# RWKV-7 and neighbourhood attention trunk: mixed inputs stored from GpSimd, two additions moved there, and the second stream's input blocks placed in reverse

## The chip, the cores and the metric

The kernel runs on one core of a Trainium2 chip. The metric is the device time of one execution in microseconds, the median of several runs. TensorE (PE) multiplies matrices; VectorE (DVE), ScalarE (ACT) and GpSimd (POOL) work element by element; SyncE (SP) issues transfers, and so does GpSimd. Each engine runs its own rows strictly in order, and waits on semaphores for what the others and the transfers have to finish first.

## The reference

Two streams (`x_prompt`, `x_sample`, each 512 tokens of width 1024) pass two layers. The change lies in the first steps of layer 0:

```python
def _rms_norm(x, g):
    y = x32 * lax.rsqrt(jnp.mean(x32 * x32, axis=-1, keepdims=True) + RMS_EPS) * g
...
def _rwkv7_branch(xn, mu, w_r, w_k, w_v, w_z, ...):
    x_prev = jnp.pad(xn[:, :-1], ((0, 0), (1, 0), (0, 0)))
    x_next = jnp.pad(xn[:, 1:], ((0, 0), (0, 1), (0, 0)))
    xx = 0.5 * (x_prev + x_next) - xn
    lerp = lambda j: xn + xx * mu[j]
    r = heads(lerp(0) @ w_r)
    k = heads(lerp(1) @ w_k)
    v = heads(lerp(2) @ w_v)
    z = xn @ w_z
    ...
    for d in range(2):      # forward and backward
        ...                 # decay and learning rate from two low-rank products
        ys.append(_wkv7_scan(r, decay, k_d, v, -kk, kk * a, reverse=(d == 1)))
    ...
    return (y * silu(z)) @ w_o
```

Layer 1 is a neighbourhood attention on a grid of 8 x 64 tokens with a gate, and each layer sits between two RMS norms. All is in float32.

## The kernel before, in words

Everything lies transposed: a block is 128 channels by 512 tokens (256 KB), and a stream's x has eight blocks. A product in float32 is made of three matmuls, of a high and a low half of either factor (`whi`, `wlo` for the weights, split by ACT and DVE from the loaded `raw`; L457 to L459 in the prelude, L937 to L939 later). A column is one block of an output: 8 x 3 matmuls, then a copy by ACT and a store to a DRAM tile (`dz`, `dk`, `dr`, `dv`).

The **prelude** comes first. `prelude(0)` normalises stream 0. `prelude(1)` does the same for stream 1, by these steps: it loads x into eight tiles `xn`; ACT squares each block and L472 adds the squares into `acc`; L485 sums over channels on PE; L490 to L499 take the root, the reciprocal and spread it on PE; L568 scales the blocks; L575 adds each token's two neighbours into `xx`. Then `mixed` makes 32 mixed inputs: eight for v of stream 0, and three (k, r, v) for each block of stream 1. Of each, ACT makes the first half (L701), DVE the second (L704), into a place of the ring `ls`, which has four places, and L353 stores it to a DRAM tile (`dlk`, `dlr`, `dlv`, with the stream and block as digits); the normalised x itself is stored for z (`dlz`). All of these are loaded again later as inputs of products. Meanwhile PE makes the columns of z, then k, then r for stream 0. The tiles `xn`, `xx`, `ls` and a few more lie in a memory pool of their own.

The order of rows on each engine in the prelude is set by a scheduler, which follows its own timeline of costs and dependences. When the prelude's code is through, its pool is closed, and the **scan phase** takes the same memory for its own tiles: `k`, `rb`, `r`, `sz`, `MT` and more. A load into such a tile has to wait until the prelude's tile that lay there has been read for the last time. The scan phase's order is woven by hand and by a planner; its first steps are the loads of `rb` and `k` for the first pair of heads, and L1012, which multiplies them on DVE.

A store goes to SP's queue in the prelude (other than the r columns', which come when the scan phase has begun in program order and `away` is set: these go to GpSimd's).

Of the kernel before, what the change touches and what calls it, by code (L numbers as in the profile page):

```python
# [12 lines left out]
F32 = mybir.dt.float32  # L13
F32R = mybir.dt.float32r
AF = mybir.ActivationFunctionType
ALU = mybir.AluOpType
# [4 lines left out]
P = 128  # L21
T = 512
D = 1024
KT = D // P
# [230 lines left out]
class Trunk:  # L255
# [97 lines left out]
        self.store(kind).dma_start(d, src)  # L353

    def store(self, kind):
        return self.nc.gpsimd if kind == "hid" or self.away and kind not in ("y", "x1", "h") else self.nc.sync

    def load(self, dst, src):
        self.nc.sync.dma_start(dst, src)
# [172 lines left out]
    def prelude(self, s):  # L532
        nc = self.nc
        vt, gps, act = nc.vector, nc.gpsimd, nc.scalar
        xs = []
        if s == 0:
            self.vectors()
        for k in range(KT):
            if s == 0 and k == self.WFIRST:
                self.first = [self.weight(self.a["w_z"][0])]  # L540
            t = self.t("xn", (P, T + 2), 16, F32, self.lp)
            self.load(t[:, 1:T + 1], self.a["x"][s][k * P:(k + 1) * P, :])
            xs.append(t)
            if s == 0:

                lo, hi = self.pair()
                act.activation(hi, t[:, 1:T + 1], AF.Identity, scale=self.vec("pre0", k))
                vt.scalar_tensor_tensor(lo, t[:, 1:T + 1], self.vec("pre0", k), hi.bitcast(F32), op0=ALU.mult, op1=ALU.subtract)
                self.xz.append((hi, lo))
                yield  # L550
        if s == 0:
            self.consts()
        acc = self.t("acc") if s else self.t("vs", bufs=self.NVS)
        for k, t in enumerate(xs):
            gps.memset(t[:, 0:1], 0.0)
            gps.memset(t[:, T + 1:T + 2], 0.0)
            self.sumsq(acc, t[:, 1:T + 1], k, vt if s or k % 2 else vt)
            yield
        for _ in range(s * self.HOLD):
            yield  # L560
        rstd = self.rstd(acc, (lambda: self.mm) if s else None)
        if s == 0:
            self.rstd0 = rstd
        yield
        xn, xx = [], []
        for k, t in enumerate(xs):
            x = t[:, 1:T + 1]
            vt.scalar_tensor_tensor(x, x, self.vec("pre0", k), rstd, op0=ALU.mult, op1=ALU.mult)  # L568
            xn.append(x)
            yield  # L570
        if s == 0:
            yield from self.lora_weights()
        for k, t in enumerate(xs):
            u = self.t("xx", (P, T), 16, F32, self.lp)
            vt.tensor_tensor(u, t[:, 2:T + 2], t[:, 0:T], op=ALU.add)  # L575
            xx.append(u)
            yield
        self.shift[s] = xn, xx

        if s:  # L580
            for k in range(KT):
                self.mixed(0, "v", 2, k, self.mm)
                yield
            for k in range(KT):
                for kind, j in (("k", 1), ("r", 0), ("v", 2)):
                    self.mixed(s, kind, j, k)
                    yield
                self.save("lz", s, k, xn[k])
            return
        pm = self.p("pf", (P, 2, T))  # L590
        ps = (self.p("pm"), self.p("us"))
        for k in range(KT):
            hi, lo = self.xz[k]
            for q2 in range(2):
                for out, w in ((pm[:, q2], self.wm), (ps[q2], self.wl)):
                    a, b = (m[:, k % 4] for m in w[2 * q2 + k // 4])
                    nc.tensor.matmul(out, a, hi, start=(k == 0), stop=False)
                    nc.tensor.matmul(out, a, lo, start=False, stop=False)
                    nc.tensor.matmul(out, b, hi, start=False, stop=(k == KT - 1))
                yield  # L600
        for k in range(KT):
            hi, lo = (self.t("lw", (P, 4, 2, 64), 16, F32R, self.lp).rearrange("p k q c -> p (k q c)") for _ in range(2))
            t = self.t("xr", bufs=self.NXR)
            self.lerp(t, xn[k], xx[k], 8 + k)
            self.xk.append(self.halves(t, lo, hi))
            yield
        for q2 in range(2):
            mw = self.t("lm", (P, T + 2), 1, F32, self.lp)
            lr = self.t("lr", (P, KT * P), 1, F32, self.lp)
            y, u = lr[:, 0:T], lr[0:64, T:2 * T]  # L610
            gps.memset(mw[:, 0:1], 0.0)
            gps.memset(mw[:, T + 1:T + 2], 0.0)
            vt.tensor_tensor(mw[:, 1:T + 1], pm[:, q2], rstd, op=ALU.mult)
            vt.tensor_tensor(y, mw[:, 2:T + 2], mw[:, 0:T], op=ALU.add)
            yield
            vt.scalar_tensor_tensor(mw[:, 1:T + 1], y, 0.5, mw[:, 1:T + 1], op0=ALU.mult, op1=ALU.subtract)
            vt.tensor_tensor(y, ps[q2], rstd, op=ALU.mult)
            vt.tensor_tensor(y, y, mw[:, 1:T + 1], op=ALU.add)
            for q in (2 * q2, 2 * q2 + 1):
                act.activation(u, y[64 * (q % 2):64 * (q % 2) + 64], AF.Tanh if q < 2 else AF.Copy)  # L620
                self.hidden(q, u)
            yield

    def mixed(self, s, kind, j, k, past=None):

        xn, xx = self.shift[s]
        t = self.t("ls", (P, T), 4, F32, self.lp)
        self.lerp(t, xn[k], xx[k], 8 * j + k, past)
        self.save("l" + kind, s, k, t)

# [1453 lines left out]
```

## Time and profile before

| | |
|---|---|
| median of three runs | 1604.6 us (1599.76 to 1607.57) |
| profiled execution | 1611.46 us, span 1609.7 us |
| PE busy | 1514.1 us, 94% of the span |
| VectorE busy | 1221.7 us, 76% |
| ScalarE busy | 968.9 us, 60% |
| GpSimd busy | 199.9 us, 12% |
| moved by DMA | 343.61 MB, 213 GB/s |

PE is busy nearly all the time. The page's share of an engine is a mean over the whole span; the prelude, to which the change belongs, ends at about 168 us, so views of that stretch alone say more than the page. In a timeline row stand start, length, engine, line and operation, and in brackets how long the engine stood idle before it and what released it. A tile's name is followed by the name of what is read; `d` ahead of a name marks its DRAM tile.

### The profile page before, as it was taken

How to read it: one execution, taken by the hardware profiler on the slowest of the kernel's cores; microseconds unless marked ns; L12 is line 12 of the kernel's file. 1: busy time of each engine (PE TensorE's matmuls, PEld its weight loads, DVE VectorE, ACT ScalarE, POOL GpSimd, SP SyncE). 2: the span in 40 equal slices, each digit the busy share in tenths (PEclk: the TensorE clock that was granted, in tenths of full speed). 3: DMA queues.
4: the chain of work that ended last, by engine and by line, in shares of the span. 5: the costliest groups of instructions: out<-in, count | busy, mean ns of one | idle time of the engine just before them, and what ended most of it. 6: DMA issues, size and time to landing. Idle time of an engine off the chain costs nothing.

```text
span 1609.7 us, 46432 instructions
## 1 busy us (share of the span) xinstructions
PE 1514.1 (94%) x18756; PEld 1171.0 (73%) x18756; DVE 1221.7 (76%) x2714; ACT 968.9 (60%) x1931; POOL 199.9 (12%) x368
## 2 busy tenths in 40 slices
PE   7988789998898999988999999999999999999998
PEld 6866667666676776766777777777777788777776
DVE  8986579678889798877899899665767585664664
ACT  6667455855747566665577665444667665464562
POOL 0000114301111012131001011000110002111110
PEclk9999899999999999999999999999999999999999
DMA  7359677766676788669678675565865347665553
GB/s 244 105 176 319 199 257 246 236 217 214 220 250 221 224 266 262 207 210 299 215 245 284 222 231 190 165 212 167 284 221 178 116 152 231 217 194 189 170 171 111
DMA packets 183670, 343.61 MB, mean 213 GB/s; under 512 B 25888, under 2 KB 58912, under 8 KB 183456
## 3 DMA queue, kind: packets, MB, share of 16 engines
q1 hardware_dynamic: 158272, 256.75, 49.9%
q0 software_dynamic: 25184, 83.90, 14.6%
q8 instruction: 147, 2.41, 0.6%
q14 instruction: 67, 0.55, 0.1%
HBM read 230.33 MB, written 107.09 MB: 210 GB/s over the span
## 4 chain that ended last, share of the span: by engine, by line
PE 58%; DVE 7%; DMA 5%; ACT 4%; issue 3%; SPq 0%; DVEq 0%; ACTq 0%
PE pg L459 7%; PE pg L457 6%; PE pg L458 6%; PE pm L937 6%; PE pm L938 4%; PE pm L939 4%; PE pf L1249 2%; PE sc L1588 2%; PE po L1621 2%; PE pt L1606 2%; PE us L1368 2%; PE zy L1321 2%; PE zy L1372 1%; PE us L1348 1%; DMA cab<-dab 1%
## 5 line engine op out<-in xcount | busy, mean ns | idle before, releaser
L937 PE MATMUL pm<-act,whi 128*128 128x512 f32 x672 | 296.7, 442 | 9.4 <-issue 4.8
L939 PE MATMUL pm<-act,wlo 128*128 128x512 f32 x672 | 268.3, 399 | 13.6 <-DVE wlo L858 13.6
L938 PE MATMUL pm<-act,whi 128*128 128x512 f32 x672 | 268.5, 400 | 4.4 <-DVE act L884 4.3
L937 PEld LDWEIGHTS pm<-act,whi 128*128 128x128 f32 x672 | 128.7, 192 | 49.5 <-issue 14.1
L939 PEld LDWEIGHTS pm<-act,wlo 128*128 128x128 f32 x672 | 129.0, 192 | 44.8 <-DVE wlo L858 15.8
L457 PE MATMUL pg<-act,whi 128*128 128x512 f32 x384 | 156.5, 408 | 0.0
L407 DVE TENSOR_TENSOR wlo<-raw,whi 128x512 fp32r<-128x512 f32 x150 | 102.7, 688 | 68.9 <-ACT whi L406 63.5
L459 PE MATMUL pg<-act,wlo 128*128 128x512 f32 x384 | 153.0, 398 | 0.0
L406 ACT CAST whi<-raw 128x512 fp32r<-128x512 f32 x150 | 92.4, 617 | 99.6 <-PE pg L458 64.4
L458 PE MATMUL pg<-act,whi 128*128 128x512 f32 x384 | 152.3, 397 | 0.0
L938 PEld LDWEIGHTS pm<-act,whi 128*128 128x128 f32 x672 | 129.6, 193 | 29.9 <-DVE act L884 6.8
L858 DVE TENSOR_TENSOR wlo<-raw,whi 128x512 fp32r<-128x512 f32 x166 | 113.4, 684 | 33.6 <-ACT whi L856 31.8
L856 ACT CAST whi<-raw 128x512 fp32r<-128x512 f32 x166 | 102.2, 619 | 36.6 <-PE pm L938 29.4
L459 PEld LDWEIGHTS pg<-act,wlo 128*128 128x128 f32 x384 | 72.2, 188 | 18.2 <-issue 4.3
L1148 DVE TENSOR_TENSOR N<-etmp,N 128x30 f32<-128x30 f32 (+14 forms) x240 | 78.8, 328 | 4.6
L1146 DVE TENSOR_TENSOR etmp<-N 128x30 f32<-128x30 f32 (+14 forms) x240 | 78.6, 328 | 4.4
L458 PEld LDWEIGHTS pg<-act,whi 128*128 128x128 f32 x384 | 72.4, 189 | 13.0 <-issue 1.0
L457 PEld LDWEIGHTS pg<-act,whi 128*128 128x128 f32 x384 | 72.2, 188 | 12.5 <-issue 0.7
L1602 ACT ACTIVATE sb<-sb,mx 128x256 f32<-128x256 f32 x128 | 64.1, 502 | 20.7 <-DVE mx L1601 20.1
L1249 PE MATMUL pf<-cab 64*64 64x128 f32 (+1 forms) x2048 | 69.4, 270 | 1.5 <-issue 1.5
L1360 ACT COPY X<-us 64x256 f32<-64x256 f32 x128 | 46.8, 366 | 27.6 <-PE zy L1227 23.7
L1031 ACT ACTIVATE th<-pm,dv 128x512 f32<-128x512 f32 x64 | 43.9, 686 | 30.3 <-PE pm L1028 29.8
(404 smaller groups left out, 3502.8 us busy)
## 6 DMA issues: line engine op xcount, KB each, us to landing
dab<-ab POOLq DMA_DIRECT2D x32, 1024.0 KB, 7.2
cab<-dab SPq DMA_DIRECT2D x64, 512.0 KB
raw<-in_w_in_dram SPq DMA_DIRECT2D x128, 256.0 KB
bias<-in_rpb_dram SPq DMA_DIRECT2D x32, 384.0 KB
raw<-in_w_z_dram SPq DMA_DIRECT2D x32, 256.0 KB
raw<-in_w_k_dram SPq DMA_DIRECT2D x32, 256.0 KB
raw<-in_w_r_dram SPq DMA_DIRECT2D x32, 256.0 KB
k<-dk SPq DMA_DIRECT2D x32, 256.0 KB
```

What stands on the lines that cost most here:

```text
L406: self.nc.scalar.copy(hi, src)
L407: (eng or self.nc.vector).tensor_tensor(lo, src, hi.bitcast(F32), op=ALU.subtract)
L457: nc.tensor.matmul(ps, hi, x[k][0], start=(k == 0), stop=False)
L458: nc.tensor.matmul(ps, hi, x[k][1], start=False, stop=False)
L459: self.mm = nc.tensor.matmul(ps, lo, x[k][0], start=False, stop=(k == KT - 1))
L856: nc.scalar.copy(hi, raw[h])
L858: nc.vector.tensor_tensor(lo, raw.pop(h), hi.bitcast(F32), op=ALU.subtract)
L937: nc.tensor.matmul(ps, hi[:, at], xh, start=(k == 0), stop=False)
L938: nc.tensor.matmul(ps, hi[:, at], xl, start=False, stop=False)
L939: nc.tensor.matmul(ps, lo[:, at], xh, start=False, stop=(k == KT - 1))
L1148: vt.tensor_tensor(N[:, q + 1:, :q], tv, N[:, q + 1:, :q], op=ALU.add)
L1249: end = nc.tensor.matmul(st.f[half(a), h, 0, d, g] if st.last else st.f[half(a), h, :, d, g], ab[half(h), d, g, 2 * e[d] + 1 - a], rt if s ...
```

## The change

Four things change, all in the prelude:

- Stores of the kinds `lk`, `lr`, `lv` and `lz` (40 transfers of 256 KB) go to GpSimd's queue instead of SP's.
- For stream 1, the squares' additions (seven) and the neighbours' (eight) run on GpSimd instead of VectorE.
- Stream 1's blocks get the eight `xn` places in opposite order: block 0 lies where block 7 lay.
- The ring `ls` has five places instead of four.

```diff
     def store(self, kind):
-        return self.nc.gpsimd if kind == "hid" or self.away and kind not in ("y", "x1", "h") else self.nc.sync
+        return self.nc.gpsimd if kind in ("hid", "lk", "lr", "lv", "lz") or self.away and kind not in ("y", "x1", "h") else self.nc.sync
...
+        spots = [self.t("xn", (P, T + 2), 16, F32, self.lp) for _ in range(KT)][::-1] if s else None
         for k in range(KT):
             if s == 0 and k == self.WFIRST:
                 self.first = [self.weight(self.a["w_z"][0])]
-            t = self.t("xn", (P, T + 2), 16, F32, self.lp)
+            t = spots[k] if s else self.t("xn", (P, T + 2), 16, F32, self.lp)
...
-            self.sumsq(acc, t[:, 1:T + 1], k, vt if s or k % 2 else vt)
+            self.sumsq(acc, t[:, 1:T + 1], k, gps if s else vt)
...
-            vt.tensor_tensor(u, t[:, 2:T + 2], t[:, 0:T], op=ALU.add)
+            (gps if s else vt).tensor_tensor(u, t[:, 2:T + 2], t[:, 0:T], op=ALU.add)
...
     def mixed(self, s, kind, j, k, past=None):
-        t = self.t("ls", (P, T), 4, F32, self.lp)
+        t = self.t("ls", (P, T), 5, F32, self.lp)
```

The line numbers of the changed kernel are one higher from L538 on. The names below carry running numbers; the digits in the name of a DRAM tile are stream and block.

On SP, at the end of the prelude, the stores of mixed inputs stand between the loads in the kernel before:

```order
L353 DMA dlv15_382_1473<-ls_381_1470 128x512
L353 DMA dlk16_387_1491<-ls_386_1488 128x512
L353 DMA dlr16_389_1499<-ls_388_1496 128x512
L353 DMA dlv16_391_1507<-ls_390_1504 128x512
L353 DMA dlk17_394_1517<-ls_393_1514 128x512
L353 DMA dlr17_399_1531<-ls_398_1528 128x512
L353 DMA dlv17_408_1552<-ls_407_1549 128x512
L359 DMA rb_453_1714<-drn0_446_1706 64x512 x2
L359 DMA k_451_1712<-dk00_217_949 128x512
L359 DMA r_452_1713<-dr00_442_1683 128x512
```

At the same place in the changed kernel, SP has the loads alone:

```order
L359 DMA raw_463_1764<-in_w_r_dram 128x512
L359 DMA drn0_446_1706<-tmp_438_1672 128x64
L359 DMA raw_470_1790<-in_w_r_dram 128x512
L359 DMA rb_453_1714<-drn0_446_1706 64x512 x2
L359 DMA k_451_1712<-dk00_217_949 128x512
L359 DMA r_452_1713<-dr00_442_1683 128x512
```

The stores are no longer ahead of `rb` and `k`. On GpSimd, whose only transfers there were the stores of r columns (`dr`), they now stand before and behind these:

```order
L353 DMA dlk12_336_1335<-ls_335_1332 128x512
L353 DMA dr00_442_1683<-tmp_441_1681 128x512
L353 DMA dlr12_347_1360<-ls_346_1357 128x512
L353 DMA dlv12_349_1368<-ls_348_1365 128x512
L353 DMA dlk13_352_1378<-ls_351_1375 128x512
L353 DMA dlr13_356_1394<-ls_355_1391 128x512
L353 DMA dr01_462_1744<-tmp_461_1742 128x512
L353 DMA dlv13_358_1402<-ls_357_1399 128x512
L353 DMA dlk14_361_1412<-ls_360_1409 128x512
L353 DMA dlr14_363_1420<-ls_362_1417 128x512
```

Ten more stores follow behind the last row shown, then the memsets of `MT` and the store of r column 2. Ahead of all, GpSimd has the additions: the squares' (L472, in a row with a library row ahead of the first), then eight pairs of a neighbours' addition and the store of that block for z:

```order
L472 TENSOR_TENSOR acc_185_798<-tmp_202_875,acc_185_798 128x512
L576 TENSOR_TENSOR xx_252_1072<-xn_184_789 128x512
L353 DMA dlz10_324_1298<-xn_184_789 128x512
L576 TENSOR_TENSOR xx_253_1077<-xn_183_788 128x512
L353 DMA dlz11_334_1330<-xn_183_788 128x512
```

The first store of a mixed input comes after the eighth pair. On PE, L485 (the sum of squares over channels) stood right ahead of the spreading L499, among the sums of a k column (L759):

```order
L459 MATMUL zy_251_1064<-lw_156_706,wlo_250_1061 128x512
L485 MATMUL pm_229_976<-ones_145,acc_185_798 128x1 x4
L499 MATMUL pm_232_989<-tmp_231_984,ones_145 128x128
L759 MATMUL pm_233_1006<-tmp_218_951,cc_143 32x128 x4
L499 MATMUL pm_232_989<-tmp_231_984,ones_145 128x128 x3
```

It now stands inside the column before (`zy_228`, with `zy_251` still to come), 38 rows earlier, while L499 keeps its place:

```order
L459 MATMUL zy_228_972<-lw_141_656,wlo_225_965 128x512
L457 MATMUL zy_228_972<-lw_144_666,whi_224_964 128x512
L485 MATMUL pm_229_976<-ones_145,acc_185_798 128x1 x4
L458 MATMUL zy_228_972<-lw_145_667,whi_224_964 128x512
L459 MATMUL zy_228_972<-lw_144_666,wlo_225_965 128x512
```

So some 38 matmuls now stand between the sum and its use. From the border to the scan phase on, the rows of PE, VectorE and ScalarE are the same in both kernels.

## The prediction

> **What bounds the kernel now.** I read the view of windows first, since the change touches only the first 170 of 1609.7 us: behind them TensorE, VectorE and ScalarE have the same rows in the same order in both kernels, and whatever is won or lost before is carried through as it is. Each row gives a stretch, its length, and busy time and instructions of PE, PEld, DVE, ACT and POOL, then granted clock, DMA share and GB/s.
>
> ```profile
> 40.00:80.00 40.00, 40.00 (x177) 32.94 (x176) 38.86 (x64) 26.22 (x46) 0.13 (x2) 1.00 0.33 106
> 80.00:120.00 40.00, 35.63 (x179) 27.17 (x177) 36.25 (x62) 27.79 (x50) 0.00 (x0) 0.91 0.51 174
> 120.00:160.00 40.00, 36.18 (x176) 26.90 (x168) 25.06 (x39) 28.68 (x51) 3.03 (x3) 1.00 0.92 319
> 160.00:200.00 40.00, 30.30 (x237) 23.37 (x238) 21.15 (x30) 18.64 (x38) 7.12 (x12) 0.83 0.59 193
> ```
>
> From 40 to 80 PE never stands. Then it loses 4.4 us, 3.8 us and 9.7 us of each 40, while the DMA engines go from half busy to 0.92. VectorE is nearly full up to 117 us and has room afterwards; GpSimd has almost nothing to do. So the last two rows are where a transfer can be the limit. The view of waits on PE, 150 to 200 us (total, times, longest):
>
> ```profile
> PE pm L939 <- DVE wlo L858: 13.0, 2, 11.5
> ```
>
> One stall of 11.5 us at the border between prelude and scan, the largest here. The releaser named is a weight's low half, so I read the timeline of all engines there (start, length, what, idle before it and releaser):
>
> ```profile
> 158.41 1.49 ACT L701 ACTIVATE ls<-xn,dv 128x512 f32<-128x512 f32 x2 [0.41 <-DMA dlk<-ls]
> 159.17 1.52 DVE L704 SCALAR_TENSOR_TENSOR ls<-xx,dv,ls 128x512 f32<-128x512 f32 x2 [0.38 <-ACT ls L701]
> 160.71 0.32 SPq L353 DMA_DIRECT2D dlv<-ls  x1
> 161.14 1.16 SPq L359 DMA_DIRECT2D rb<-drn  x2
> 162.35 0.58 SPq L359 DMA_DIRECT2D k<-dk  x1
> 166.40 0.75 DVE L1012 SCALAR_TENSOR_TENSOR rb<-k,cv,rb 128x512 f32<-128x512 f32 x1 [3.76 <-DMA k<-dk]
> 167.07 0.69 DVE L858 TENSOR_TENSOR wlo<-raw,whi 128x512 fp32r<-128x512 f32 x1
> 167.81 0.79 PE L939 MATMUL pm<-act,wlo 128*128 128x512 f32 x1 [11.48 <-DVE wlo L858]
> ```
>
> The weight itself is not late: L858 stands on VectorE behind L1012, which waits 3.76 us for the load of k; that load stands on SP behind the two loads of rb, these behind the last store of a mixed input, and that behind the last mixed input (ACT L701, then DVE L704). The stall ends when the last of the 32 mixed inputs is done, plus 2.45 us on SP (159.90 to 162.35) and 4.05 us until k is used. Why the last one is so late, the view of the tile ls says:
>
> ```profile
> L701 ACT ACTIVATE ls<-xn,dv x32: 711/724/732, 106.5 to 159.2; 128x512 f32<-128x512 f32 x32
> L704 DVE SCALAR_TENSOR_TENSOR ls<-xx,dv,ls x32: 737/750/754, 111.9 to 159.9; 128x512 f32<-128x512 f32 x32
> L353 SPq DMA_DIRECT2D dlv<-ls x16: 319/388/470, 113.7 to 160.7; - x16
> ...
>   DMA dlv<-ls: 8.7, 8
> ...
>   DMA dlr<-ls: 1.5, 2
>   DMA dlk<-ls: 0.6, 2
> ```
>
> The last rows are idle time of ACT ahead of L701: 10.8 us in 12 waits for a place that a store hasn't left. 32 stores take 47.0 us (113.7 to 160.7), 1.5 us each, though one is issued in 0.39 us: it is a ring of four places against transfers and whatever stands ahead on SP.
>
> **The change part by part.** The remaining rows, first of the two additions that leave VectorE, the scaling ahead of the second, and the stores of z (count, durations in ns, first and last start):
>
> ```profile
> L472 DVE TENSOR_TENSOR acc<-tmp,acc x7: 679/682/686, 74.3 to 91.2; 128x512 f32<-128x512 f32 x7
> L575 DVE TENSOR_TENSOR xx<-xn x8: 682/683/684, 109.5 to 116.3; 128x512 f32<-128x512 f32 x8
> L568 DVE SCALAR_TENSOR_TENSOR xn<-xn,cv,acc x8: 744/746/754, 104.1 to 108.8; 128x512 f32<-128x512 f32 x8
> L353 SPq DMA_DIRECT2D dlz<-xn x8: 319/320/432, 105.1 to 109.6; - x8
> ```
>
> then GpSimd's own timeline up to the border, and the landing of its stores of r (min, median, max):
>
> ```profile
> 74.49 0.10 POOL L611 MEMSET lm<- 128x1 f32 x1 [72.56 <-DVE lr L618]
> ...
> 148.57 0.68 POOL L353 DMA_DIRECT2D dr<-tmp  x1 [73.95 <-ACT tmp L745]
> 154.56 0.54 POOL L353 DMA_DIRECT2D dr<-tmp  x1 [5.31 <-ACT tmp L745]
> 155.09 1.83 POOL L1815 MEMSET MT<- 128x2048 f32 x1
> 160.74 1.82 POOL L1815 MEMSET MT<- 128x2048 f32 x1 [3.83 <-DVE ls L704]
> 162.56 0.54 POOL L353 DMA_DIRECT2D dr<-tmp  x1
> ```
>
> ```profile
> DMA to landing us min/median/max: 2.3/4.1/5.6
> ```
>
> *Price of an addition on GpSimd.* No row of before has GpSimd read the SBUF. Below, an addition can't be priced under the memset of a tile of 512, 1.83/4 = 0.46 us; above, two reads and a write one after the other at that pace are 1.37 us. I take 1.37, since nothing shows that the passes overlap. The Trainium skill (GPSIMD Engine Reference, section 3.1) gives 4497 ns for an addition of 2048 elements, which would be an estimated 1.12 us here; by it every sum below with 1.37 is some 2 to 4 us too long on GpSimd, and none changes its sign.
>
> *Seven additions of squares.* VectorE loses 7 x 0.682 = 4.8 us of work in a stretch where it is full. On GpSimd they take 9.6 us. PE's L485, which sums the result, stands 38 rows earlier on PE, and at 40.00/177 = 0.226 us a row (first window above) that is 8.6 us: 88.2 us instead of 96.80. From 74.3 to 88.2 there is room for 13.9 us, 1.99 us for each addition; at 1.37 PE doesn't wait. GpSimd's library row costs nothing: it is among the first rows, inside the idle 72.56 us. What L485's new place does, this timeline of PE says:
>
> ```profile
> 96.80 0.94 PE L485 MATMUL pm<-ones,acc 128*128 128x1 f32 x8
> 99.68 0.46 PE L499 MATMUL pm<-tmp,ones 128*128 128x128 f32 x2 [1.94 <-DVE tmp L495]
> 102.94 0.66 PE L759 MATMUL pm<-tmp,cc 128*32 128x128 f32 x8 [1.58 <-ACT tmp L754]
> ```
>
> ```profile
> PE pm L759 <- ACT tmp L754: 2.4, 2, 1.6
> ```
>
> The 1.94 us go, since root, reciprocal and diagonal are made under the matmuls that now follow L485. The 1.58 us have another cause (the square of a k column, L754) and stay; the other wait of this kind, 2.4 - 1.6 = 0.8 us by the view of waits for 80 to 160 us, is at one of two sums that move a column later on PE, and I leave its gain out as small. The clock may give more: two windows,
>
> ```profile
> 98.00:104.00 6.00, 2.74 (x25) 1.87 (x26) 2.46 (x8) 5.18 (x12) 0.00 (x0) 0.83 0.26 87
> 104.00:117.00 13.00, 13.00 (x53) 9.98 (x53) 12.97 (x22) 8.02 (x15) 0.00 (x0) 0.82 0.67 246
> ```
>
> lose 6 x 0.17 + 13 x 0.18 = 3.4 us of full speed. Whether the lower clock comes of the stall, before alone can't say; its ends are 0 and 3.4, and I take 1, nearer to nothing, since one of the two waits about there remains. So PE comes to the columns of r 2.9, say 3 us earlier, and the store of r column 1, made from PE's result, goes from 154.56 to 151.6.
>
> *Eight additions of neighbours, and z.* VectorE loses another 5.5 us, GpSimd gets eight pairs, addition and store of z: 8 x (1.37 + 0.54) = 15.3 us. All stand ahead of its first store of a mixed input. With the scaling 3 us earlier (101.1 + 0.75) the pairs end at 117.2, so the first of these stores goes 3.5 us later than now (113.7). Behind it ACT waits, once five places are full; the 1.5 us per store of today hold 10.8 us of such waiting, which is room to catch up in, so I cost this at nothing. If that cover is gone, it is the third rival.
>
> *Stores on GpSimd.* SP loses 40 issues, and its weights, loads of k and rb pass them: nothing waits there any more for a mixed input to be made. For the weights that wins nothing: of the 3.82 us that PE loses from 120 to 160, 3.67 are the start of the stall (its last matmul ends at 156.33, 11.48 ahead of 167.81). But the queue on GpSimd is in order too. Between the stores of mixed inputs now stand those of r columns 0 and 1, each waiting for PE and ACT. Thirteen stores (of 32) are behind r column 1, four more between the two. Before, SP sent the last twelve (counted in its timeline, the first of them here) from 146.05 to 160.71, 1.33 us apart:
>
> ```profile
> 146.05 0.32 SPq L353 DMA_DIRECT2D dlk<-ls  x1
> ```
>
> The two MT memsets come behind all stores, 1.83 us each; they were held by VectorE's last mixed input anyway (3.83 us), and r column 2's store after them moves with them, ahead of nothing at the border.
>
> *Five places, and the tail.* This is the term that decides. Take r column 1's store at D, a landing of L after its issue. The first five of the thirteen are ready and go at D + 0.54. The sixth input waits for the first landing: its store goes at D + 0.54 + L + 0.72 + 0.75 = D + 2.0 + L. The eleventh waits for that: D + 2.0 + 2L, and eleventh to thirteenth take ACT 3 x 0.72, so ACT is done at D + 4.2 + 2L. In the changed order the load of k needs just that (its memory is x block 7, the last read, in the place that was block 0's), neither the store nor rb behind it. So k is loaded at D + 4.2 + 2L against 162.35 now. With D = 151.6 and L = 2.3: 160.4, 2.0 us won. With 4.1: 164.0, 1.6 us lost. Between these, 3.2 gives 162.2, nothing. I take a bit below 3.2, since PE stands then and asks for no weights: 2.8, k at 161.4, 1 us won. The landing of k (4.05 us) stays as it is.
>
> *Reversed places* by themselves cost no instruction: block 7 now lies where k's tile comes, block 6 where rb's, and the scaling and mixing go through the blocks in the same order as before.
>
> **The sum.** +0 (squares) +0 (neighbours, under the wait for places) -3 at PE, of which the tail lets through -1, since PE then only comes sooner to the same stall, which is 2 us longer. The profiled execution took 1611.46 us (span 1609.7), so it would be 1610.5; it is 6.9 us above the median of the three runs, 1604.6, and against that the forecast is 1603.6. Half a per cent, 8 us, is about what a measurement of this kernel tells from no change, so this is no change.
>
> **The rivals.**
> *1. The tail runs free (faster).* If the clock's whole 3.4 us come back, D = 154.56 - 1.94 - 3.4 = 149.2; with L = 2.3, k is loaded at 158.0, 4.4 us sooner, and lands in 2.3 instead of 4.05: 6.1 us won, 1598.5. At most the whole stall, 11.5 us, 1593.1. For it: the DMA engines have 8% left only because all is pressed in after 117 us. Against: the two r stores.
> *2. The queue on GpSimd holds the ring (slower).* PE isn't sooner (D = 154.56) and a store lands in 4.1 to 5.6: k at 167.0 to 170.0, 4.6 to 7.6 us lost, 1609.2 to 1612.2. It decides from D + 4.2 + 2L = 162.35 on, so at L above 1.8 if PE isn't sooner, above 3.3 if it is. For it: median 4.1. Against: these landings come from all over the span.
> *3. GpSimd's additions are slow or hold VectorE up (slower).* Above 1.99 us per addition PE waits at L485, 0.7 us for each tenth more. Pairs above 2.2 us move the first store past 119.5, from where 31 further stores at 1.33 us end later than 160.7. If each addition stopped VectorE for its own length, VectorE, full up to 117 us, would have 15 x 1.37 = 20.6 us less and 10.3 us back: up to 10 us late, 1614.6. The Trainium skill (SBUF - State Buffer, "Who interferes with whom") has this rule: a VectorE instruction with two SBUF inputs and a GpSimd one that reads SBUF share a lock. No row here shows either.
>
> **How the numbers follow.** Forecast (between 4 us won and 3 lost, 1600.6 to 1607.6): 0.45. Rival 1: 0.25; rival 2: 0.18; rival 3: 0.12. The range runs from the whole stall won, 1593, to 1613, which leaves out a part of rival 3 and whatever else is unknown. Faster by over 0.5% needs rival 1 beyond its worked case, or more than the stall: most of its 0.25. Slower needs rival 3 or the upper end of 2: together 0.19. The rest, 0.56, is no change.
>
> **What would show it.** On PE: L499 without a wait and L485 about 88 us; L939 at the border still with a stall, 9 to 14 us, behind L1012 and the load of k. On GpSimd: additions of 1 to 1.4 us, two idle stretches ahead of the r stores, then a run of stores. On ACT: waits ahead of L702 for stores still, now longest around r column 1. Wrong would be: a stall under 6 us (rival 1), the load of k after 165 us (2), VectorE's instructions stretched beyond 0.75 us between 74 and 117 us (3).

## The result, and the profile after

| | before | changed |
|---|---|---|
| median of 11 runs each | 1606.98 us | 1616.0 us |
| ratio | | 1.0055 (95% interval 1.0036 to 1.0074) |
| profiled execution, span | 1609.7 us | 1612.6 us |
| PE goes on behind its largest stall ("the border") | 167.81 us | 171.93 us |

The change costs 0.55%, about 9 us; the forecast was no change at 1603.6, so it missed, and the interval excludes no change. The two profiled executions lie only 2.9 us apart because that of before was a long one among its runs and that of the change a short one. So I measure by the border, and by timed ratios.

The windows of 40 us, as quoted for before (stretch, length, busy time and instructions of PE, PEld, DVE, ACT, POOL, clock, DMA share, GB/s), now of the changed kernel:

```profile
80.00:120.00 40.00, 34.55 (x170) 26.13 (x168) 39.08 (x48) 25.47 (x46) 20.05 (x23) 0.96 0.44 147
120.00:160.00 40.00, 37.18 (x176) 28.43 (x176) 22.04 (x35) 25.84 (x48) 12.22 (x23) 0.96 0.87 304
160.00:200.00 40.00, 26.46 (x226) 20.87 (x226) 23.43 (x36) 21.95 (x42) 12.63 (x20) 0.83 0.59 201
```

From 80 to 120 VectorE is busier than before (39.08 instead of 36.25 us) with fewer instructions (48 instead of 62), though work was taken off it. And the DMA engines carry less: share 0.44 instead of 0.51, then 0.87 instead of 0.92. The view of waits on PE from 60 to 172 us:

```profile
PE pm L940 <- DVE wlo L859: 13.4, 1, 13.4
PE pm L760 <- ACT tmp L755: 3.6, 1, 3.6
PE zy L459 <- DVE wlo L407: 2.4, 1, 2.4
```

L499 has no wait any more. But the wait for the k column's square (L760) has grown from 1.6 to 3.6 us, a weight is late in a k column (2.4 us), and the stall at the border is 13.4 us. At the border the timeline of all engines has:

```profile
165.71 0.72 ACT L702 ACTIVATE ls<-xn,dv 128x512 f32<-128x512 f32 x1 [1.12 <-DMA dlk<-ls]
166.50 0.33 SPq L359 DMA_DIRECT2D k<-dk  x1
170.52 0.75 DVE L1013 SCALAR_TENSOR_TENSOR rb<-k,cv,rb 128x512 f32<-128x512 f32 x1 [3.04 <-DMA k<-dk]
171.93 0.80 PE L940 MATMUL pm<-act,wlo 128*128 128x512 f32 x1 [13.38 <-DVE wlo L859]
```

The load of k does follow ACT's half of the last mixed input directly now (166.43 to 166.50, against 2.45 us before). But that half is done 6.5 us later: 166.43 instead of 159.90. (Both times are the end of ACT's row. VectorE's half ends 0.8 us later in either kernel, and the prediction's "done" at 159.90 is ACT's.) Where the inputs lose it, GpSimd's timeline shows:

```profile
103.82 1.48 POOL L576 TENSOR_TENSOR xx<-xn 128x512 f32<-128x512 f32 x1 [18.83 <-DVE xn L569]
...
105.96 1.05 POOL L576 TENSOR_TENSOR xx<-xn 128x512 f32<-128x512 f32 x1
106.94 0.56 POOL L353 DMA_DIRECT2D dlz<-xn  x1
...
117.46 1.08 POOL L353 DMA_DIRECT2D dlv<-ls  x2
119.08 1.87 POOL L353 DMA_DIRECT2D dlv<-ls  x3 [0.55 <-DVE ls L705]
133.81 0.54 POOL L353 DMA_DIRECT2D dlv<-ls  x1 [12.85 <-DVE ls L705]
```

After the eight pairs, five stores go, and then GpSimd stands 12.85 us for the sixth mixed input. VectorE's timeline in that stretch:

```profile
114.32 3.21 DVE L705 SCALAR_TENSOR_TENSOR ls<-xx,dv,ls 128x512 f32<-128x512 f32 x2
117.45 0.68 DVE L407 TENSOR_TENSOR wlo<-raw,whi 128x512 fp32r<-128x512 f32 x1
118.05 2.06 DVE L705 SCALAR_TENSOR_TENSOR ls<-xx,dv,ls 128x512 f32<-128x512 f32 x3
120.04 1.28 DVE L407 TENSOR_TENSOR wlo<-raw,whi 128x512 fp32r<-128x512 f32 x2
122.53 0.69 DVE L407 TENSOR_TENSOR wlo<-raw,whi 128x512 fp32r<-128x512 f32 x1 [1.22 <-ACT whi L406]
127.13 0.69 DVE L407 TENSOR_TENSOR wlo<-raw,whi 128x512 fp32r<-128x512 f32 x1 [3.90 <-ACT whi L406]
128.77 0.69 DVE L407 TENSOR_TENSOR wlo<-raw,whi 128x512 fp32r<-128x512 f32 x1 [0.95 <-ACT whi L406]
132.13 0.69 DVE L407 TENSOR_TENSOR wlo<-raw,whi 128x512 fp32r<-128x512 f32 x1 [2.66 <-ACT whi L406]
132.75 0.75 DVE L705 SCALAR_TENSOR_TENSOR ls<-xx,dv,ls 128x512 f32<-128x512 f32 x1
```

Between the fifth and the sixth mixed input stand six halves of weights (L407, 120.04 to 132.13), and each of the last four waits for its high half on ACT. ACT stands in turn: from 105 to 136 us it waits 9.1 us, in two waits, for a k weight's load and 5.5 us, in five, for PE to give weight places back. The loads again wait on SP for VectorE to have read the weight ahead (19.2 us from 100 to 140 us, 0.4 us before). ACT's half of the sixth input has the same six weights ahead of it in ACT's order and starts at 132.00, with no wait of its own. A place in the ring was there sooner: the first store was issued at 117.46, and the first five landed 3.2 to 5.7 us after their issue, so by 123.2 us at the latest. So the sixth input waits for its turn in the order, at weight speed. In VectorE's order this is written down:

```order
L705 SCALAR_TENSOR_TENSOR ls_291_1200<-xx_98_409,dv_147,ls_291_1200 128x512
L407 TENSOR_TENSOR wlo_338_1338<-raw_321_1289,whi_337_1337 128x512
L407 TENSOR_TENSOR wlo_342_1346<-raw_339_1341,whi_341_1345 128x512
L407 TENSOR_TENSOR wlo_344_1350<-raw_340_1343,whi_343_1349 128x512
L407 TENSOR_TENSOR wlo_372_1441<-raw_369_1436,whi_371_1440 128x512
L407 TENSOR_TENSOR wlo_374_1445<-raw_370_1438,whi_373_1444 128x512
L407 TENSOR_TENSOR wlo_403_1538<-raw_400_1533,whi_402_1537 128x512
L705 SCALAR_TENSOR_TENSOR ls_293_1208<-xx_99_414,dv_147,ls_293_1208 128x512
```

`ls_291` is the fifth. Before, two halves stood between the fourth and the fifth and none between fifth and sixth, which VectorE made at once:

```profile
117.53 1.28 DVE L407 TENSOR_TENSOR wlo<-raw,whi 128x512 fp32r<-128x512 f32 x2
118.73 1.41 DVE L704 SCALAR_TENSOR_TENSOR ls<-xx,dv,ls 128x512 f32<-128x512 f32 x2
```

Windows cut to the stretch (columns as above) show what it does to the transfers, here in the changed kernel:

```profile
104.00:117.00 13.00, 13.00 (x61) 9.95 (x62) 13.00 (x9) 7.74 (x14) 12.71 (x16) 0.87 0.48 181
117.00:135.00 18.00, 15.56 (x77) 11.04 (x77) 7.85 (x13) 6.41 (x13) 3.70 (x7) 0.91 0.74 247
```

Before, the first of these had a DMA share of 0.67 (quoted ahead), and the second 0.91:

```profile
117.00:135.00 18.00, 17.01 (x87) 11.43 (x87) 12.03 (x18) 12.22 (x23) 0.00 (x0) 1.00 0.91 313
```

The inputs missed here are made later. The border is the same matmul in both kernels. PE comes to the stall ahead of it at 158.55 us, against 156.33 before, and then stands 13.38 instead of 11.48 us: of the 4.1 us at the border 2.2 are lost on the way and 1.9 in the stall.

### The profile page after: what moved, and what is told of

It reads as the page before. It is cut to its first block, busy times and chain, and to the rows that moved or that the text cites. A ratio compares the mean times of both kernels' runs of the same rounds, so it can differ in the third digit from the quotient of the medians.

```text
span 1612.6 us, 46450 instructions
## 1 busy us (share of the span) xinstructions
PE 1505.3 (93%) x18756; PEld 1163.5 (72%) x18756; DVE 1224.8 (76%) x2699; ACT 967.8 (60%) x1931; POOL 241.6 (15%) x423
## 4 chain that ended last, share of the span: by engine, by line
PE 63%; DVE 12%; DMA 9%; issue 8%; ACT 6%; POOL 2%; SPq 1%; DVEq 0%; POOLq 0%; ACTq 0%
PE pg L459 7%; PE pg L457 6%; PE pg L458 6%; PE pm L938 6%; PE pm L940 5%; PE pm L939 5%; PE pf L1250 3%; PE sc L1589 2%; PE po L1622 2%; PE pt L1607 2%; PE us L1369 2%; PE zy L1322 2%; PE us L1349 2%; DVE wlo L859 1%; PE zy L1373 1%
## 5 line engine op out<-in xcount | busy, mean ns | idle before, releaser
L407 DVE TENSOR_TENSOR wlo<-raw,whi 128x512 fp32r<-128x512 f32 x150 | 104.0, 695 | 73.4 <-ACT whi L406 68.2
L1349 PEld LDWEIGHTS us<-Z,MT 64*64 64x64 f32 x1024 | 37.3, 135 | 31.5 <-ACT Z L1334 17.9
```

The source lines that it names most:

```text
L407: (eng or self.nc.vector).tensor_tensor(lo, src, hi.bitcast(F32), op=ALU.subtract)
```

## The experiments

Fifteen changed kernels, each against the kernel before on the same chip. The border is from one profile each; the ratio is of all timed runs, with its 95% interval.

| kernel | stores on GpSimd | squares | neighbours | places reversed, ring | border us | ratio |
|---|---|---|---|---|---|---|
| changed | all 40 | GpSimd | GpSimd | yes, 5 | 171.93 | 1.0055 (1.0036 to 1.0074) |
| e1_no_adds | all 40 | VectorE | VectorE | yes, 5 | 163.68 | 0.9998 (0.9979 to 1.0017) |
| e2_adds_only | none | GpSimd | GpSimd | no, 4 | 168.84 | 0.9990 (0.9969 to 1.0010) |
| e3_stores_only | all 40 | VectorE | VectorE | no, 4 | 165.51 | 1.0033 (1.0015 to 1.0051) |
| e4_places_ring | none | VectorE | VectorE | yes, 5 | 164.60 | 1.0001 (0.9983 to 1.0019) |
| e5_no_neighbours | all 40 | GpSimd | VectorE | yes, 5 | 163.75 | 0.9966 (0.9947 to 0.9985) |
| e5_again | as e5 | | | | 163.17 | 0.9976 (0.9955 to 0.9997) |
| e6_no_squares | all 40 | VectorE | GpSimd | yes, 5 | 174.38 | 1.0048 (1.0025 to 1.0072) |
| e7_r_on_sp | all 40, two r on SP | GpSimd | GpSimd | yes, 5 | 172.16 | 1.0058 (1.0037 to 1.0078) |
| e8_no_stores | none | GpSimd | GpSimd | yes, 5 | 162.95 | 0.9975 (0.9956 to 0.9994) |
| e9_first8_on_sp | 32 | GpSimd | GpSimd | yes, 5 | 170.24 | 1.0003 (0.9984 to 1.0022) |
| e10_z_on_sp | 32 | GpSimd | GpSimd | yes, 5 | 165.22 | 1.0005 (0.9990 to 1.0021) |
| e12_squares_ring | none | GpSimd | VectorE | yes, 5 | 165.93 | 1.0019 (1.0004 to 1.0035) |
| f4_ring4 | all 40 | GpSimd | GpSimd | yes, 4 | 177.69 | 1.0055 (1.0032 to 1.0078) |
| g2_v_first | none | GpSimd | GpSimd | yes, 5 | 164.85 | 0.9970 (0.9953 to 0.9988) |
| g3_v_first_queue | all 40 | GpSimd | VectorE | yes, 5 | 162.30 | 0.9962 (0.9943 to 0.9981) |
| e0_before_again | as before | | | | 165.57 | one run |

**e0.** The kernel before once more (no edit), for how far a border repeats.

> The kernel before once more, for a second profile: how far the border (167.8 us) and the rest of the span (1441.9 us) repeat. Expected: the border within 0.7 us; the rest within 6 us, since the granted clock of runs goes from 0.976 to 0.985.

165.57 against 167.81: a border moves by 2.2 us from run to run, three times what I expected; the rest of the span repeated (1443.3 and 1441.9 us). So single borders that differ by 2 us say nothing. Over these fifteen kernels and the one before (entered as 166.7 and 1; e5 as the mean of both its rows) border and time go together, correlation 0.82, and 1 us of border is 0.94 us of time: on the whole, what happens ahead of the border is carried through. Single kernels stray from that line (e3, f4).

**e1.** The change without its additions:

```diff
-            self.sumsq(acc, t[:, 1:T + 1], k, gps if s else vt)
+            self.sumsq(acc, t[:, 1:T + 1], k, vt if s or k % 2 else vt)
-            (gps if s else vt).tensor_tensor(u, t[:, 2:T + 2], t[:, 0:T], op=ALU.add)
+            vt.tensor_tensor(u, t[:, 2:T + 2], t[:, 0:T], op=ALU.add)
```

> The change without the two additions on GpSimd (both stay on VectorE); stores on GpSimd, reversed places and five places stay. Theory 1 (the additions are the loss: each stops VectorE for its own length, 15 instructions of VectorE stretched to 1.5 to 1.8 us, so weights and mixed inputs come late, and the order made round them puts mixed inputs behind r's stores): no VectorE instruction above 0.8 us, PE back at the border (after its largest stall) at 161 to 165 us instead of 171.9, and the kernel 3 to 6 us faster than before (0.996 to 0.998). Theory 2 (the queue on GpSimd is the loss: a mixed input's store waits behind a store of an r column): the border stays at 168 to 172 and the kernel stays slower, 1.002 to 1.006.

The border came where theory 1 has it, and the loss is gone; a gain did not show in the ratio. So the additions are needed for the loss, and the stores alone with the r columns' in their queue are not it.

**e2.** Before, with the two lines of the diff for `sumsq` and `xx` alone.

> The kernel before with the two additions on GpSimd alone; stores stay on SP, four places, old order of places. Theory 1: VectorE's scaling of x takes 1.4 us a block instead of 0.75, the border comes at 171 to 175 us and the kernel is slower by 4 to 9 us (1.0025 to 1.0055), the whole loss of the change. Theory 2: the additions are covered, border within 1 us of 167.8, ratio 1.000.

No loss, though VectorE is stopped just as in the change. The scaling of the eight blocks in its timeline, in e2 and then in the change:

```profile
103.12 10.09 DVE L568 SCALAR_TENSOR_TENSOR xn<-xn,cv,acc 128x512 f32<-128x512 f32 x8
```

```profile
102.99 11.41 DVE L569 SCALAR_TENSOR_TENSOR xn<-xn,cv,acc 128x512 f32<-128x512 f32 x8
```

Before it took 5.39 us. Theory 1 has its mechanism right and its price wrong: additions without the stores cost nothing that can be measured, in the old places and with a ring of four.

**e3.** Before, with the line of `store` alone.

> The kernel before with the 40 stores on GpSimd alone; four places. Theory 1: without the additions the stores do little harm; the load of k is no longer behind the last store but in the old places it waits for other blocks; border 165 to 169 us, ratio 0.998 to 1.001. Theory 2: eight stores stand behind r column 1's in GpSimd's order, with four places the ring is held there, border 170 to 173 us, ratio 1.002 to 1.005.

A border 2.3 us (or nothing, by e0) ahead of before's and a ratio above 1: the one kernel whose time and border disagree by more than their uncertainty. Its runs had the lowest mean granted clock of those timed with it (0.9798; 0.9825 to 0.9829 in the three others and in the kernel before), but why its clock should be lower is open.

**e4.** Before, with the lines of `spots` and the ring of five alone.

> The kernel before with reversed places and five places for mixed inputs alone; additions on VectorE, stores on SP. Both theories: one more place takes some of the 10.8 us of ACT's waits for stores away, yet the load of k stays behind the last store on SP; border 165 to 168 us, ratio 0.998 to 1.000. If the border comes at 171 or later, both are wrong and the places are the loss.

As expected in time; the border a bit sooner. Here the scheduler put the load of k ahead of that of rb, and of most of the queue: k is issued at 155.89, and the releaser named is now rb.

**e5, e5 again.** The change with the neighbours' line undone:

```diff
-            (gps if s else vt).tensor_tensor(u, t[:, 2:T + 2], t[:, 0:T], op=ALU.add)
+            vt.tensor_tensor(u, t[:, 2:T + 2], t[:, 0:T], op=ALU.add)
```

> The change with the neighbours' additions back on VectorE; the squares' stay on GpSimd, as do stores, places and ring. Theory 3 (the neighbours' additions and the stores share one queue: eight pairs stand ahead of the first store of a mixed input, and the order made round that leaves 13 of 32 stores behind r column 1's instead of 4): here 4 stand behind it, border at 162 to 165 us, ratio 0.998 to 1.001. Theory 1 (any addition on GpSimd stops VectorE, and the seven squares weigh as much as the eight neighbours): border 167 to 170, ratio 1.002 to 1.004.

> The change without the neighbours' additions on GpSimd, once more, for whether its 0.9966 repeats: border within 1 us of 163.7, ratio 0.995 to 0.999. If 0.999 to 1.001, the first figure was luck and only the loss of the three kernels with the neighbours' additions and all stores on GpSimd stands.

The loss is gone and 4 stores stand behind r column 1's, as theory 3 has it, with a gain on top, 0.34% and 0.24%. (e7 shows that it is not these stores' place that decides.) The transfers start where the change has its pairs; windows of e5:

```profile
104.00:117.00 13.00, 12.94 (x61) 9.89 (x62) 13.00 (x21) 8.48 (x16) 6.28 (x12) 0.87 0.80 284
117.00:135.00 18.00, 16.82 (x88) 11.83 (x87) 12.35 (x19) 12.81 (x24) 6.70 (x13) 1.00 0.95 324
```

DMA share 0.80 and 0.95, against 0.48 and 0.74 in the change.

**e6.** The change with the squares' line undone:

```diff
-            self.sumsq(acc, t[:, 1:T + 1], k, gps if s else vt)
+            self.sumsq(acc, t[:, 1:T + 1], k, vt if s or k % 2 else vt)
```

> The change with the squares' additions back on VectorE; the neighbours' stay on GpSimd. Theory 3: as the whole change, 14 stores behind r column 1's, border 171 to 174 us, ratio 1.004 to 1.007. Theory 1: about half of the loss, border 167 to 170, 1.002 to 1.004.

The whole loss is there without the squares. The seven additions of theory 1 that run beside a full VectorE from 73 to 85 us cost nothing that can be measured.

**e7.** The change, with the first two r stores out of GpSimd's queue:

```diff
-        self.store(kind).dma_start(d, src)
+        self.store("y" if kind == "r" and s == 0 and p < 2 else kind).dma_start(d, src)
```

> The whole change, but the stores of r columns 0 and 1 go to SP's queue, so that no mixed input's store stands behind them on GpSimd. Theory 2 (these two in the queue hold the ring): border 165 to 168 us, ratio 1.000 to 1.003. Theory 3 (the order of mixed inputs on ACT and VectorE is late by itself, whatever the queue): border within 1.5 us of 171.9, ratio 1.004 to 1.007.

This rejects theory 2, on which my prediction's main term rested. GpSimd's idle stretch and SP's load of k stand where the change has them:

```profile
133.84 0.54 POOL L353 DMA_DIRECT2D dlv<-ls  x1 [12.84 <-DVE ls L705]
```

```profile
153.35 0.32 SPq L353 DMA_DIRECT2D dr<-tmp  x1
...
165.84 0.33 SPq L359 DMA_DIRECT2D k<-dk  x1
```

**e8.** The change with the line of `store` undone (all stores on SP).

> The change with the 40 stores back on SP; additions on GpSimd, reversed places and five places stay. Additions alone gave 0.999, places and ring alone 1.0001. Theory 3: no loss without the shared queue, border 165 to 169 us, ratio 0.998 to 1.001. If the loss comes of additions with the new places, border 171 or later and 1.004 or more.

No loss, and a gain of 0.25%. In its order no more than two weight halves stand between one mixed input and the next, VectorE makes 11 inputs from 113.1 to 129.8 us where the change makes five, and the DMA share from 117 to 135 us is 0.98.

**e9 and e10.** The change, with eight of its stores left on SP: those of stream 0's inputs (e9), or those of z (e10).

```diff
 # e9
-        self.store(kind).dma_start(d, src)
+        self.store("y" if kind == "lv" and s == 0 else kind).dma_start(d, src)
 # e10
-        return self.nc.gpsimd if kind in ("hid", "lk", "lr", "lv", "lz") or ...
+        return self.nc.gpsimd if kind in ("hid", "lk", "lr", "lv") or ...
```

> The whole change, but the eight stores of stream 0's mixed inputs (dlv0) stay on SP; both additions on GpSimd, the stores of z and of stream 1's inputs too. Theory 3b (the loss is the place of these eight in GpSimd's queue, behind eight pairs of addition and store: the ring is full after five, so the order on VectorE has six weight splits, each waiting for its load, between the fifth and the sixth mixed input): here no such run of splits, no idle stretch above 5 us on GpSimd, DMA share from 104 to 135 us above 0.75, border 162 to 165 us, ratio 0.996 to 0.999. Theory 1 (VectorE stopped by the additions is the loss): its scaling still takes 11.4 us, border 169 to 172, ratio 1.003 to 1.006.

> The whole change, but the eight stores of z stay on SP, so that GpSimd has the eight additions alone ahead of the first mixed input. Theory 3b: the first of these goes 8 x 0.54 = 4 us sooner, three splits instead of six stand ahead of the sixth input, border 163 to 167 us, ratio 0.997 to 1.001. Theory 1: as the whole change, 1.004 to 1.006.

Either takes the loss away (1.0003, 1.0005), with both additions still on GpSimd. In e9 the run of six halves is gone and the share from 117 to 135 us is 0.98, though VectorE's scaling takes 11.41 us as in the change. But it misses the rest: GpSimd still stood 7.43 us, the share from 104 to 117 us was 0.46, so that over both stretches it is 0.76, and the border came at 170.24, not 162 to 165. In e10 three halves stand ahead of the sixth input, as expected, and it is made at 123.37. So the run of halves is most of the loss by the ratios, and not all that makes a border late.

**e12.** Squares on GpSimd, places and ring, all stores on SP, neighbours on VectorE.

> The squares' additions on GpSimd, reversed places and five places; all stores on SP, the neighbours' additions on VectorE. If the squares are what gains (the change without neighbours gave 0.9966 with them, 0.9998 without), this has the gain without any store on GpSimd: border 162 to 164.5 us, ratio 0.995 to 0.998. If the gain needs the stores off SP: 0.999 to 1.001.

Not a gain, rather a small loss. e5's gain needs the stores off SP; the squares alone don't bring it.

**f4.** The whole change with a ring of four:

```diff
-        t = self.t("ls", (P, T), 5, F32, self.lp)
+        t = self.t("ls", (P, T), 4, F32, self.lp)
```

> The whole change with four places for mixed inputs instead of five. Theory 3b (the ring is full while GpSimd's queue is at its pairs, so a run of weight splits, each behind its load, stands in VectorE's order ahead of the next mixed input): the run comes after the fourth input instead of the fifth, so all are later: idle stretch on GpSimd again 12 us or more, border 173 to 176 us, ratio 1.006 to 1.010. Theory 1 (VectorE stopped by the additions): the ring doesn't matter, 171 to 172.5 and 1.004 to 1.007.

The run of six halves comes after the fourth input, and GpSimd's idle stretch is again 12.84 us: the run's place follows the ring, as 3b says. The border is 6 us later than the change's, more than expected, and the ratio 1.0055, lower than expected (its interval reaches 1.0078): the last microseconds of border are not in the time here.

**g2 and g3.** The eight inputs of stream 0 are written ahead of stream 1's neighbours' additions (in e8's kernel and in e5's):

```diff
+        if s:
+            for k in range(KT):
+                self.mixed(0, "v", 2, k, self.mm)
+                yield
         for k, t in enumerate(xs):
             u = self.t("xx", (P, T), 16, F32, self.lp)
...
-            for k in range(KT):
-                self.mixed(0, "v", 2, k, self.mm)
-                yield
```

> Both additions on GpSimd, reversed places, five places, all stores on SP as in the run that gave 0.9975, and the eight mixed inputs of stream 0 written ahead of stream 1's additions, so that they are made while VectorE's order still has room. Theory 3b: transfers start some 10 us sooner, DMA share from 104 to 117 us above 0.70, border 159 to 163 us, ratio 0.993 to 0.998. If the border moves and the ratio does not (0.998 to 1.002), time won ahead of the border is not carried through.

> Stores on GpSimd, squares' additions on GpSimd, neighbours' on VectorE (the kernel that gave 0.9966), and the eight mixed inputs of stream 0 written ahead of stream 1's additions. Theory 3b: DMA share from 104 to 117 us at 0.80 or above, border 160 to 164 us, ratio 0.993 to 0.998.

Both are faster than before, g3 by 0.38%, the lowest ratio of all. But neither differs clearly from the kernel that it was made from (e8 0.9975, e5 0.9966 and 0.9976): the intervals overlap. The windows of g3 show the transfers nearly full 13 us sooner:

```profile
104.00:117.00 13.00, 12.02 (x57) 9.19 (x58) 12.87 (x21) 9.69 (x18) 6.81 (x13) 0.87 0.99 363
```

and its stall at the border is 2.55 us; what is left ahead of the border is now PE's own work and its waits in the k columns. g2's border missed (164.85, not 159 to 163).

## Why the prediction was wrong, point by point

**The failed step** is in "Eight additions of neighbours, and z": the stores' late start was costed at nothing, because ACT's 10.8 us of waits for a place were taken as "room to catch up in". The start itself was sized well: 117.46 us, 117.2 forecast. But the room was not there: in the changed order six weight halves stand between the fifth and the sixth mixed input, and the sixth comes at 132.75, against 119.39 before. In the end the last input is 6.5 us later. Over all kernels the orders divide in the same way: six halves follow each other in the change, e6, e7 and f4, whose next input comes at 132.0 to 133.6 us, and these four have the loss; in the kernel before and the eleven others there are at most three (e10, g2), mostly two. e5, e8, e9 and e10 each take away a part of what fills that queue, and each loses the loss; e6 and e7 leave it there and keep the loss; f4 moves it by one input, with the ring one place smaller. That the scheduler took the ring for full at that point is read from this; its own timeline is in no view here. That the run of halves was in the changed order, and open to be read, is the lesson: I showed the orders of stores and of PE, and not the one of the engine that makes what is stored.

**The tail** (load of k at D + 4.2 + 2L) named the wrong holder. The r stores in the queue were to set it; e7 took them out and k was loaded at 165.84 instead of 166.50. With the thirteen inputs late by themselves, D had next to no part in it. With the measured D of 153.58 and median landing of 3.8 us the formula gives 165.4: that this is near 166.50, and that rival 2's 167.0 is, is chance.

**PE 3 us sooner** did not come. L485 ran at 88.69 (88.2 forecast) and L499 had no wait, as said, but PE then waited 3.62 us for the next square of a k column, L760, where it had waited 1.58: the stall went to the next late thing. r column 1's store left at 153.58, against 154.56 before, but in a second run of before it left at 151.62 (e0). And PE came to the stall at the border at 158.55, against 156.33 and 154.48 (e0): instead of 3 us won, 2 to 4 lost.

**Price of an addition**: among the neighbours' 1.05 us where VectorE left GpSimd alone and 1.48 where it did not, so 1.37 was in between and the pairs took 13.6 us, not 15.3. The squares' took 1.35 to 1.72 us beside the full VectorE, below the 1.99 from which PE would wait. **Reversed places and the load of k**: right, k follows the last input at once; that is 2.4 us won which the change gives back.

**Rivals.** Two of the signs of being wrong came: the load of k after 165 us and VectorE's instructions stretched. Rival 2, to which the first belongs, is rejected by e7. Of rival 3 the second mechanism is there: VectorE's instructions beside an addition took 1.64 to 1.79 us instead of 0.68 to 0.75, as the Trainium skill (SBUF - State Buffer, "Who interferes with whom") has it for two SBUF inputs on VectorE and a reading GpSimd; the trace agrees, 1.67 = 0.68 + about 1.0. But its price was wrong: 10.1 us instead of 5.39 for the scaling, in e2, e8 and e10, goes with ratios of 0.9990, 0.9975 and 1.0005, and 11.41 in e9 with 1.0003. So it is chance that its "up to 10 us late" is near the 9 us measured. It has a share all the same: behind the stretched scaling the first weight half comes at 117.45 instead of 114.39, and the next k weight's load at 118.16, and from there on the run of six goes at weight speed. What decides is not that VectorE is stopped, but what its order puts behind.

What stays open: of some 9 us, single borders show 4.1 (e0: up to 6.4); the borders of the four kernels with the loss are 171.9 to 177.7, those of the others 162 to 170. The rest of the span was 1437 to 1443 us in the four and 1435 to 1453 in the others, at clocks of 0.977 to 0.985, so no further place of loss is to be seen in it, nor excluded below some 3 us. The mean granted clock of the timed runs goes with the ratios too: 0.9795 to 0.9799 in e6, e7 and f4, 0.9831 to 0.9850 in e5, e8, g2 and g3, 0.9816 and 0.9817 in the runs of before timed with them. At about 1 us for each 0.001 (last section) that is an estimated 2 us of the 8 to 9 lost, and 1.4 to 3.4 us of the 4 to 6 won, so the gains may be in good part the clock's; whether a kernel's order sets its clock is open. e3's loss of 0.33%, without a run of halves and with a border ahead of before's, has no place in its profile, and its clock would be an estimated half of it. No run changes VectorE's order alone with the queues as they are, which would test the run of halves directly.

## What to carry to other kernels

When a change moves stores to another queue, read in the changed order not only the queue, but the order of the engine that fills the ring: here the order put other work ahead of the ring's next input, and that work's waits became the ring's. Put nothing long in a queue ahead of the stores that free a small ring; here eight stores moved elsewhere turned 0.55% of loss into none, and so did leaving the neighbours' additions on VectorE, with 0.2 to 0.3% of gain, of which the clock may be a part. An engine stopped by another is no loss by itself, if what waits behind it has cover.

## What the runs showed of the hardware

An addition of 128 x 512 with two inputs in SBUF took 1.05 us on GpSimd when VectorE left it alone, and 1.35 to 1.72 us beside a busy VectorE (the change). A VectorE instruction with two SBUF inputs beside it took 1.64 to 1.79 us instead of 0.68 to 0.75, nearly the sum of both, and one of the eight scalings 3.36 us. Beside the same additions a VectorE addition that reads one input straight from a product of PE (L732, at 75.14 us) took 0.68 us as before.

Two executions of one kernel differ by 2.2 us at the border, 166 us into the program. Whole runs of the kernel before took 1600 to 1613 us in one set of 35 and up to 1619 us in another, longer the lower their mean granted clock: 0.6 to 1.2 us for each 0.001 of clock in four sets of 29 to 35 runs, correlation -0.40 to -0.76.
